# Moving the background modulation products out of two weight groups and into the first column blocks of the output projection

## The chip, the cores and the metric

The kernel runs on one core of one Trainium2 chip. The metric is the device time of one execution in microseconds (us); the core's TensorE (PE), VectorE (DVE), ScalarE (ACT), GpSimd (POOL) and the queue of SyncE (SP), which issues nearly all transfers, work side by side, each through its own instructions in a fixed order.

## What is computed

One layer of a streaming encoder on 512 tokens of width 2048, in float32. What matters here, cut from the reference:

```
cond = silu(c)
mod  = cond @ ada_w + ada_b                     # (2048,) @ (2048, 12288)
sh_m, sc_m, gt_m, sh_f, sc_f, gt_f = split(mod, 6)
h = rms_norm(x, mix_pre_g) * (1 + sc_m) + sh_m
(a_q ... d_v) = split(h @ w_in)                 # four mixers: delta rule, two attentions, spatial gate
y = concat(out_a, out_b, out_c, out_d) @ w_out  # output projection
x = x + gt_m * rms_norm(y, mix_post_g)
h = rms_norm(x, ffn_pre_g) * (1 + sc_f) + sh_f
x = x + gt_f * rms_norm(conv_glu_ffn(h), ffn_post_g)
```

## The kernel before, in words

Every large product is done in three matmuls of a split operand: a weight tile is loaded (`raw`, 512 KB to a unit), ACT rounds it to `hi`, DVE takes `lo = raw - hi`, and PE adds hi\*hi, lo\*hi and hi\*lo. Units come through `wunit` (line 351 is the load, 376 the `hi`, 377 the `lo`). Four `raw` tiles and five `hi`/`lo` pairs are in turn.

The kernel first makes `h` and the early groups of the input projection (keys, queries, values and gate of the delta rule). Then the delta rule itself runs (DeltaNet below: convolutions and norms at lines 787 to 856, a triangular solve by 31 steps of two DVE operations at lines 944 and 946, a recurrence over 8 chunks at 1006 to 1044), then come the late groups of the input projection in the order bv, bk, ck, dv, bq, cq, du (L380 to L382 and L573 to L575), the attentions of mixer B (L1107 to L1129) and mixer C (L1149 to L1187), and the output projection. That is the order of the program's text. A scheduler interleaves it: on each engine the text's order gives the priority, so the late groups' matmuls fill PE while the DeltaNet chain waits for DVE and ACT. What stands in which order on an engine is fixed when the kernel is built.

The modulation `mod` is worked in the background. Of its 24 column pieces the first 8 are needed at once; the other 16 (`bg_units(range(8, 24))`, the gates and the FFN's shift and scale) are cut into 9 steps each, 144 in all. Eight are units of 512 KB (`gemv_unit`: load at L415 into one of five tiles `ada`, which odd weight units of the late groups and the rows of x in the output projection share). Units 0, 2, 4, 6 make two products each on ACT (L430, L434), which POOL adds up (L435); units 1, 3, 5, 7 make two products each on DVE (L428, L432). The ninth step adds the two sums on DVE (L439) and stores them (L692).

Steps are called in two places. In the late groups `between()` does `pace[0]` steps per weight unit, set from the table `RATE`, one number for each of the seven groups; there are 8 units in bv, bk, dv, bq, cq and du, 4 in ck. In the output projection, four column blocks (`cb`) of 8 weight units each, `bg_step` is called once per unit. At the start of column block 0 and in unit 3 of blocks 0 to 2, `gate_row` loads a finished sum (L702) with a gain and a bias (L714, L715) and spreads it by two matmuls (L705, L706) into `gt`, by which the block's result is multiplied (`yg`, L1262) before it is stored (L1263).

Of the kernel before, what the change touches and what calls it, by code (L numbers as in the profile page):

```python
# [249 lines left out]
def trunk_kernel(ctx: ExitStack, tc: tile.TileContext, a: dict, out: bass.AP):  # L250
# [30 lines left out]
    def mt(s="m", shape=(P, 512), dt=F32):  # L281
        return cur[0].tile(list(shape), dt, tag="m", name=nm(s))
# [7 lines left out]
    def acc(s="acc"):  # L290
        return pp.tile([P, 512], F32, tag="acc", name=nm(s))
# [56 lines left out]
    def wunit(src, nk, w, own=True, shadow=False):  # L348

        raw = wraw() if own else araw()  # L350
        nc.sync.dma_start(out=raw[:, :nk * w], in_=src[:, :nk * w])
        step = max(1, 512 // w)
        out_ = []
        for j in range(0, nk, step):
            m = min(step, nk - j) * w
            hi = wp.tile([P, 512], F32R, tag="hi", name=nm("hi"))
            lo = wp.tile([P, 512], F32R, tag="lo", name=nm("lo"))
            split(raw[:, j * w:j * w + m], hi[:, :m], lo[:, :m], None, shadow)
            out_ += [(hi[:, i * w:(i + 1) * w], lo[:, i * w:(i + 1) * w]) for i in range(min(step, nk - j))]
        return out_  # L360
# [45 lines left out]
    def galloc(s, dt=F32):  # L406
        if mixing_open[0]:
            return gp.tile([P, 512], dt, tag="ga", name=nm(s), bufs=NGA)
        return mt(s, dt=dt)
# [299 lines left out]
    def gate_row(c, w, o):  # L709

        ps = bg_row(c)
        gt, pg = rtile("gt"), rtile("pg")
        sl = slice(o * 512, (o + 1) * 512)
        nc.sync.dma_start(out=gt, in_=a["gtb"][:, w * D + o * 512:w * D + (o + 1) * 512].partition_broadcast(P))  # L714
        nc.sync.dma_start(out=pg, in_=a["mpg" if w == 0 else "fpg"][0:1, sl].partition_broadcast(P))  # L715
        V.tensor_tensor(gt, gt, ps, ALU.add)
        V.tensor_tensor(gt, gt, pg, ALU.mult)
        return gt
# [21 lines left out]
    def bg_step(n=1):  # L740
        for _ in range(n):
            f = next(bg, None)
            if f is None:
                return
            bgn[0] += 1
            f()
# [20 lines left out]
    def late_groups(name, rate):  # L767
        pace[0] = rate
        for g in late:
            if (g[1][0][0] if g[0] == "FM" else g[1]) == name:  # L770
                if g[0] == "FM":
                    fm_group(g, ev_late_fm)
                else:
                    tm_group(g, ev_late_tm)

    def staged(name, j):
        t = mt("sd")
        nc.sync.dma_start(out=t, in_=std[STG[name] + j])
        return t
# [267 lines left out]

    late_groups("bv", RATE[0])
    late_groups("bk", RATE[1])
    late_groups("ck", RATE[2])  # L1050
    late_groups("dv", RATE[3])

# [41 lines left out]

    late_groups("bq", RATE[4])
    for tt in range(NTT):
# [36 lines left out]
    ckt = [staged("ck", j) for j in range(2)]  # L1133
    late_groups("cq", RATE[5])
    alit = [mt("ali") for _ in range(2)]
# [58 lines left out]
    def load_mix(uk):  # L1194
        raw = wraw()
        nc.sync.dma_start(out=raw.rearrange("p (k t) -> p k t", k=2), in_=mixd[uk[0]:uk[0] + 2].rearrange("k p t -> p k t"))
        for j, kt in enumerate(uk):
            mh[kt], ml[kt] = hslot(kt, "m")
            split(raw[:, j * 512:(j + 1) * 512], mh[kt], ml[kt])
# [5 lines left out]
    def turn(ygs, tag=None):  # L1205

        for j in range(4):
            ps = pp.tile([P, 512], F32, tag=tag or mtag(), name=nm("hT"), bufs=2)
            for tt in range(NTT):
                TE.transpose(ps[:, tt * P:(tt + 1) * P], ygs[tt][:, j * P:(j + 1) * P], ident)  # L1210
            t = mt("ygT")
            S.activation(t, ps, AF.Copy)
            ygT.append(t)

    def x_sums(cb):

        xs = []
        for tt in range(NTT):
            if tt % 2 == 0:
                xw = araw()  # L1220
            xr = xw[:, tt % 2 * 512:(tt % 2 + 1) * 512]
            nc.sync.dma_start(out=xr, in_=a["x"][tt * P:(tt + 1) * P, cb * 512:(cb + 1) * 512])
            jk = galloc("jx")
            S.activation(jk, xr, AF.Square, accum_out=sy[:, 3, tt * 4 + cb:tt * 4 + cb + 1])
            xs.append(xr)
        return xs
# [3 lines left out]
    for cb in range(4):  # L1230
        gt = gts.pop(0)
        ps = None
        us = gout[cb]
        ws = {}
        for n_, (ui, (uk, uc)) in enumerate(us):
            if cb == 0 and not 8 <= uk[0] < 12:
                load_mix(uk)
            for kt, w in zip(uk, wunit(a["w_out"][ui], len(uk), 512)):
                ws[kt] = w
            if ps is None:  # L1240
                ps = [acc("y") for _ in range(NTT)]
            if n_ == 3 and cb < 3:
                gts.append(gate_row(9 + cb, 0, cb + 1))
            if n_ == 1 and prev:
                turn(prev)
            if n_ == 1:
                xs = x_sums(cb)
            if not (cb == 3 and n_ > 3):
                bg_step(2 if cb < 2 else 3)
            if n_ == len(us) - 2 and cb == 3:  # L1250
                continue
            order = [(kt, tt) for kt in uk for tt in range(NTT)]
            if n_ == len(us) - 1 and cb == 3:
                order = [(kt, tt) for tt in range(NTT) for kt in us[n_ - 1][1][0] + uk]
            for kt, tt in order:
                sl = slice(tt * P, (tt + 1) * P)
                tm_mm(ps[tt], mh[kt][:, sl], ml[kt][:, sl], ws[kt][0], ws[kt][1], kt == korder[0], kt == korder[-1])
        prev = []
        for tt in range(NTT):
            i = tt * 4 + cb  # L1260
            yg = mt("yg")
            V.tensor_tensor(yg, ps[tt], gt, ALU.mult)  # L1262
            nc.sync.dma_start(out=ygd[tt, cb], in_=yg)  # L1263
            jk = galloc("jy")
            S.activation(jk, ps[tt], AF.Square, accum_out=sy[:, 0, i:i + 1])
            V.scalar_tensor_tensor(tt_("jz"), xs[tt], 1.0, yg, ALU.mult, ALU.mult, accum_out=sy[:, 2, i:i + 1])
            S.activation(jk, yg, AF.Square, accum_out=sy[:, 1, i:i + 1])
            prev.append(yg)
        if cb == 1:
            while bgn[0] < 12 * 9:  # L1270
                bg_step()
            S.activation(st(1), epst, AF.Sqrt)
        if cb == 2:
            for c in range(12, 20):
                ff_row(c)
            ff_cols()
# [335 lines left out]
    for ui, (uk, uc) in gdn[0]:  # L1612
        raw = wraw()
        nc.sync.dma_start(out=raw, in_=a["w_dn"][ui])
        for j in range(2):
            f, cb = (uk[j], uc[0] // 512) if len(uk) == 2 else (uk[0], uc[0] // 512 + j)
# [46 lines left out]
SHADOW = (0, 1, 2, 3)  # L1663
NHL2 = 3
NADA = 5
RATE = (1, 1, 2, 2, 3, 3, 3)
NGA = 3
NBR = 5
HV = (1, 4)
# [19 lines left out]
```

## Time and profile before

| what | value |
|---|---|
| time, median of 3 runs | 2326.64 us (2321.76 to 2336.99) |
| the profiled execution's own time | 2319.29 us |
| its span | 2316.8 us |
| PE busy | 2189.0 us, 94% of the span |
| DVE, ACT, POOL busy | 73%, 63%, 46% |
| DMA | 480.24 MB, mean 207 GB/s |

The span is from the first to the last instruction; 2.5 us of the execution's time lie outside it. Busy time is summed over the whole kernel; PE's matmuls overlap, so that a busy PE is an upper bound of its work. The background steps run between 176 us and 803 us of the span; behind that comes the FFN, which the change does not touch.

### The profile page before, as it was taken

How to read it: one execution, taken by the hardware profiler on the slowest of the kernel's cores; microseconds unless marked ns; L12 is line 12 of the kernel's file. 1: busy time of each engine (PE TensorE's matmuls, PEld its weight loads, DVE VectorE, ACT ScalarE, POOL GpSimd, SP SyncE). 2: the span in 40 equal slices, each digit the busy share in tenths (PEclk: the TensorE clock that was granted, in tenths of full speed). 3: DMA queues.
4: the chain of work that ended last, by engine and by line, in shares of the span. 5: the costliest groups of instructions: out<-in, count | busy, mean ns of one | idle time of the engine just before them, and what ended most of it. 6: DMA issues, size and time to landing. Idle time of an engine off the chain costs nothing. (4 is left out here: it accounts for less than half of the span.)

```text
span 2316.8 us, 31339 instructions
## 1 busy us (share of the span) xinstructions
PE 2189.0 (94%) x9852; PEld 1734.0 (75%) x9852; DVE 1680.9 (73%) x2665; ACT 1463.4 (63%) x2638; POOL 1077.0 (46%) x848
## 2 busy tenths in 40 slices
PE   5999999989999998989999999999999999999998
PEld 3878876767677786767788887777777777877776
DVE  5887678877878545956665568788788767777777
ACT  5767465355567544666777677776776677666663
POOL 4663032243323200256445465755765765564643
PEclk8999999999999999999999999999999999999999
DMA  8876555677888754678853547456545634435333
GB/s 299 285 259 236 170 183 180 198 240 254 295 306 284 248 171 146 231 257 291 282 206 137 182 167 273 160 198 213 190 176 204 216 141 173 155 106 194 119 132 137
DMA packets 206574, 480.24 MB, mean 207 GB/s; under 512 B 32692, under 2 KB 74180, under 8 KB 206408
## 3 DMA queue, kind: packets, MB, share of 16 engines
q1 hardware_dynamic: 199576, 477.19, 59.1%
q10 hardware_dynamic: 6832, 1.06, 0.2%
q8 instruction: 78, 1.28, 0.2%
q14 instruction: 88, 0.72, 0.1%
HBM read 399.50 MB, written 78.67 MB: 206 GB/s over the span
## 5 line engine op out<-in xcount | busy, mean ns | idle before, releaser
L1481 PE MATMUL X<-hi,ah 128*128 128x512 f32 x960 | 386.8, 403 | 19.3 <-DVE c L1493 6.1
L435 POOL TENSOR_TENSOR ga<-ga,ada 128x512 f32<-128x512 f32 (+1 forms) x167 | 226.5, 1356 | 369.5 <-ACT ada L434 348.9
L1482 PE MATMUL X<-lo,ah 128*128 128x512 f32 x960 | 383.7, 400 | 1.0 <-DVE lo L1447 1.0
L1483 PE MATMUL X<-hi,al 128*128 128x512 f32 x960 | 383.4, 399 | 0.0
L1447 DVE TENSOR_TENSOR lo<-raw,hi 128x512 fp32r<-128x512 f32 x360 | 264.2, 764 | 110.7 <-ACT hi L1446 110.2
L1468 POOL TENSOR_TENSOR raw<-raw 128x512 f32<-128x512 f32 x120 | 161.9, 1353 | 319.3 <-ACT hi L1443 232.1
L1481 PE MATMUL Z<-hi,ah 128*128 128x512 f32 x720 | 286.8, 398 | 6.4 <-ACT c L1491 2.9
L1444 DVE TENSOR_TENSOR lo<-raw,sh 128x512 fp32r<-128x512 f32 x360 | 240.1, 683 | 72.2 <-ACT sh L1442 35.6
L1442 ACT ACTIVATE sh<-raw 128x512 fp32r<-128x512 f32 x360 | 210.5, 588 | 124.1 <-DMA raw<-w_dn 63.3
L1483 PE MATMUL Z<-hi,al 128*128 128x512 f32 x720 | 285.7, 397 | 0.8 <-POOL al L1418 0.8
L1482 PE MATMUL Z<-lo,ah 128*128 128x512 f32 x720 | 285.4, 396 | 0.0
L1446 ACT ACTIVATE hi<-raw 128x512 fp32r<-128x512 f32 x360 | 214.4, 625 | 95.2 <-PE X L1483 36.4
L1443 ACT ACTIVATE hi<-raw 128x512 fp32r<-128x512 f32 x360 | 221.4, 622 | 35.7 <-PE Z L1483 24.9
L1481 PEld LDWEIGHTS X<-hi,ah 128*128 128x128 f32 x960 | 183.1, 191 | 66.5 <-DVE c L1493 7.4
L380 PE MATMUL acc<-hh,hi 128*128 128x512 f32 x544 | 221.3, 410 | 9.2 <-ACT lt L764 6.7
L382 PE MATMUL acc<-hh,lo 128*128 128x512 f32 x544 | 221.5, 410 | 4.2 <-DVE lo L374 4.1
L381 PE MATMUL acc<-hl,hi 128*128 128x512 f32 x544 | 222.4, 409 | 0.4 <-POOL hl L493 0.3
L1482 PEld LDWEIGHTS X<-lo,ah 128*128 128x128 f32 x960 | 183.0, 191 | 43.2 <-DVE lo L1447 1.3
L1483 PEld LDWEIGHTS X<-hi,al 128*128 128x128 f32 x960 | 183.0, 191 | 42.7
L1481 PEld LDWEIGHTS Z<-hi,ah 128*128 128x128 f32 x720 | 135.7, 189 | 41.2 <-ACT c L1491 4.3
L432 DVE SCALAR_TENSOR_TENSOR ga<-ada,cond,ga 128x512 f32<-128x512 f32 (+1 forms) x183 | 148.7, 813 | 22.2 <-DMA ada<-ada 20.3
L376 ACT ACTIVATE hi<-raw 128x512 fp32r<-128x512 f32 (+1 forms) x162 | 97.6, 609 | 100.3 <-PE y L575 51.7
(363 smaller groups left out, 4698.0 us busy)
## 6 DMA issues: line engine op xcount, KB each, us to landing
ada<-ada SPq DMA_DIRECT2D x184, 512.0 KB, 4.6
raw<-w_up SPq DMA_DIRECT2D x172, 512.0 KB, 5.9
raw<-w_dn SPq DMA_DIRECT2D x86, 512.0 KB, 5.4
raw<-w_in SPq DMA_DIRECT2D x56, 512.0 KB, 4.4
partd<-c SPq DMA_DIRECT2D x80, 256.0 KB, 4.2
c<-partd SPq DMA_DIRECT2D x80, 256.0 KB, 3.7
actd<-q SPq DMA_DIRECT2D x40, 512.0 KB, 3.3
ar<-actd SPq DMA_DIRECT2D x35, 512.0 KB, 3.5
```

What stands on the lines that cost most here:

```text
L380: TE.matmul(o, sh, mh, start=first, stop=False)
L381: TE.matmul(o, sh, ml, start=False, stop=False)
L382: TE.matmul(o, sl, mh, start=False, stop=last)
L435: G.tensor_tensor(accs[eng], accs[eng], src, ALU.add)
L1442: S.activation(sh, src, AF.Copy)
L1443: S.activation(h_, src, AF.Copy)
L1444: V.tensor_tensor(l_, src, sh, ALU.subtract)
L1446: S.activation(h_, src, AF.Copy)
L1447: eng.tensor_tensor(l_, src, h_, ALU.subtract)
L1481: TE.matmul(ps, ah[:, sl], wh, start=st_, stop=False, skip_group_check=True)
L1482: TE.matmul(ps, ah[:, sl], wl, start=False, stop=False, skip_group_check=True)
L1483: TE.matmul(ps, al[:, sl], wh, start=False, stop=sp_, skip_group_check=True)
```

## The change

Two numbers and one condition. In `RATE` the groups bv and bk go from 1 step per weight unit to 0, so 16 steps are no longer called there. In column blocks 0 and 1 of the output projection each unit calls 3 steps in place of 2, which is 16 more. Before, 112 steps were called in the late groups and 32 in the two column blocks; now it is 96 and 48. Either way the 144th is called in the last unit of column block 1, so the calls of blocks 2 and 3 find nothing left.

```
@@ -1246,7 +1246,7 @@
             if n_ == 1:
                 xs = x_sums(cb)
             if not (cb == 3 and n_ > 3):
-                bg_step(2 if cb < 2 else 3)
+                bg_step(3)
             if n_ == len(us) - 2 and cb == 3:
                 continue
@@ -1663,7 +1663,7 @@
-RATE = (1, 1, 2, 2, 3, 3, 3)
+RATE = (0, 0, 2, 2, 3, 3, 3)
 NGA = 3
```

Since all later calls go on from where the earlier ones stopped, the same call now does a step that is 16 earlier in the list, until the output projection catches up.

On DVE, in the norms of the DeltaNet keys (`cv` is the convolution of one head, `ga` the running sum of products, `lo` a weight split of a late group; what is before has -, what is now has +):

```order
 L856 TENSOR_TENSOR kq_2558<-cv_2587,nB_2605 128x2x128
 L787 TENSOR_SCALAR cv_2609<-pa_357,colp 128x512
-L377 TENSOR_TENSOR lo_3664<-ada_3657,hi_3663 128x512
 L790 SCALAR_TENSOR_TENSOR cv_2609<-pa_357,colp,cv_2609 128x511
+L377 TENSOR_TENSOR lo_3637<-ada_3630,hi_3636 128x512
 L790 SCALAR_TENSOR_TENSOR cv_2609<-pa_357,colp,cv_2609 128x510
-L377 TENSOR_TENSOR lo_3698<-raw_3695,hi_3697 128x512
 L790 SCALAR_TENSOR_TENSOR cv_2609<-pa_357,colp,cv_2609 128x509
-L432 SCALAR_TENSOR_TENSOR ga_3875<-ada_3958,cond,ga_3875 128x512 x2
+L377 TENSOR_TENSOR lo_3667<-raw_3664,hi_3666 128x512
 L792 SCALAR_TENSOR_TENSOR cv_2609<-pa_357,cv_2609 128x512
```

Two products are gone from between the four operations of one head's convolution, and the weight splits have moved a little.

On the SP queue, at the boundary of column blocks 0 and 1 (`ada<-ada` is a load of a background unit, `raw<-w_out` of a weight unit, `ygd<-yg` the store of a result of block 0), before:

```order
L351 DMA raw_7267<-w_out 128x1024
L351 DMA raw_7311<-w_out 128x1024
L351 DMA raw_7368<-w_out 128x1024
L351 DMA raw_7413<-w_out 128x1024
L714 DMA gt_6867<-gtb 128x512
L715 DMA pg_6868<-mpg 128x512
L415 DMA ada_7239<-ada 128x1024
L702 DMA ga_7321<-accd 128x512
L1263 DMA ygd<-yg_7101 128x512
```

and now:

```order
L351 DMA raw_7148<-w_out 128x1024
L1222 DMA ada_7186<-x 128x512 x2
L1222 DMA ada_7193<-x 128x512 x2
L415 DMA ada_7200<-ada 128x1024
L1263 DMA ygd<-yg_7064 128x512
L1263 DMA ygd<-yg_7072 128x512
L1263 DMA ygd<-yg_7080 128x512
L1263 DMA ygd<-yg_7088 128x512
L415 DMA ada_7206<-ada 128x1024
L351 DMA raw_7236<-w_out 128x1024
L415 DMA ada_7246<-ada 128x1024
L415 DMA ada_7252<-ada 128x1024
```

Before, the weights of block 1 were issued up to its sixth unit ahead of the first store; now its second unit is the last ahead of the stores, and its third comes behind the four of them.

## Rows read from the trace of the kernel before

**Rows 1.** The page: busy time of each engine.

```profile
PE 2189.0 (94%) x9852; PEld 1734.0 (75%) x9852; DVE 1680.9 (73%) x2665; ACT 1463.4 (63%) x2638; POOL 1077.0 (46%) x848
```

**Rows 2.** Busy time by stage: stretch, length, engines, granted PE clock, DMA share, GB/s.

```profile
176.00:264.00 88.00, 87.66 (x427) 72.91 (x426) 58.92 (x98) 50.14 (x86) 20.09 (x16) 1.00 0.59 203
264.00:423.00 159.00, 149.19 (x755) 113.19 (x754) 126.62 (x230) 85.61 (x132) 39.42 (x29) 0.98 0.54 176
423.00:488.00 65.00, 58.29 (x242) 46.52 (x241) 62.33 (x101) 25.78 (x42) 23.86 (x15) 0.95 0.69 236
...
583.00:692.00 109.00, 103.76 (x466) 77.87 (x465) 87.67 (x171) 63.68 (x134) 32.37 (x28) 1.00 0.86 307
692.00:764.00 72.00, 62.28 (x290) 48.20 (x289) 55.65 (x127) 49.11 (x111) 20.26 (x14) 0.95 0.76 266
764.00:813.00 49.00, 49.00 (x213) 39.18 (x212) 28.71 (x46) 26.77 (x56) 11.99 (x9) 0.97 0.82 267
813.00:912.00 99.00, 98.76 (x438) 78.84 (x437) 46.01 (x84) 45.18 (x105) 0.00 (x0) 1.00 0.51 160
```

**Rows 3.** What PE waited for from 264 to 488 us.

```profile
PE acc L380 <- ACT lt L764: 6.7, 1, 6.7
PE gF L922 <- DVE tg L920: 2.6, 2, 1.9
...
PE gB L889 <- DVE tl L887: 2.5, 1, 2.5
```

**Rows 4.** ACT in order of time, 452 to 484 us: start, length, instruction, idle before.

```profile
468.75 1.33 ACT L434 ACTIVATE ada<-ada,cond 128x512 f32<-128x512 f32 x2 [3.14 <-DMA ada<-ada]
...
471.92 1.58 ACT L764 ACTIVATE lt<-acc 128x512 f32<-128x512 f32 x3
```

**Rows 5.** Groups by line, 176 to 813 us: the background operations.

```profile
L432 DVE SCALAR_TENSOR_TENSOR ga<-ada,cond,ga 128x512 f32<-128x512 f32 x118 | 105.7, 896 | 17.2 <-DMA ada<-ada 16.2
...
L439 DVE TENSOR_TENSOR ga<-ga,ga 128x512 f32<-128x512 f32 x17 | 13.2, 775 | 3.5 <-POOL ga L435 3.0
...
L428 DVE TENSOR_SCALAR ga<-ada,cond 128x512 f32<-128x512 f32 x16 | 8.8, 547 | 2.8 <-DMA ada<-ada 2.7
...
L434 ACT ACTIVATE ada<-ada,cond 128x512 f32<-128x512 f32 x116 | 79.4, 715 | 43.2 <-DMA ada<-ada 31.0 <-DVE ga L432 7.0 <-DVE lo L377 3.1
...
L435 POOL TENSOR_TENSOR ga<-ga,ada 128x512 f32<-128x512 f32 x117 | 165.1, 1411 | 306.7 <-ACT ada L434 289.4 <-DVE ga L428 7.4 <-issue 3.1
```

**Rows 6.** Groups by line on DVE in the triangular solve, 423 to 488 us.

```profile
L432 DVE SCALAR_TENSOR_TENSOR ga<-ada,cond,ga 128x512 f32<-128x512 f32 x14 | 11.4, 818 | 0.0
...
L377 DVE TENSOR_TENSOR lo<-raw,hi 128x512 fp32r<-128x512 f32 x10 | 6.8, 684 | 0.1
```

**Rows 7.** What PE waited for from 692 to 813 us.

```profile
PE cT L1168 <- DVE cp L1063: 5.3, 7, 1.6
...
PE y L575 <- DVE ml L1187: 0.9, 1, 0.9
```

**Rows 8.** DVE in order of time at the end of column block 0.

```profile
760.97 0.69 DVE L716 TENSOR_TENSOR gt<-gt,gtps 128x512 f32<-128x512 f32 x1 [5.04 <-DMA gt<-gtb]
...
762.63 0.68 DVE L1187 TENSOR_TENSOR ml<-oc,mh 128x512 fp32r<-128x512 f32 x1
```

**Rows 9.** The SP queue in order of time there.

```profile
764.92 0.92 SPq L1263 DMA_DIRECT2D ygd<-yg  x2
...
767.34 0.92 SPq L1263 DMA_DIRECT2D ygd<-yg  x2
```

**Rows 10.** Transfers issued from 764 to 813 us: count, KB each, median us to landing.

```profile
ada<-ada SPq DMA_DIRECT2D x10, 512.0 KB, 3.6
raw<-w_out SPq DMA_DIRECT2D x8, 512.0 KB, 6.6
```

**Rows 11.** The fastest stretches for DMA in this part (columns as in rows 2).

```profile
660.00:690.00 30.00, 29.19 (x129) 21.79 (x128) 24.29 (x54) 19.48 (x43) 7.29 (x6) 1.00 0.91 323
...
680.00:692.00 12.00, 12.00 (x58) 9.41 (x57) 8.68 (x28) 7.46 (x21) 0.65 (x1) 1.00 1.01 364
```

More of the change, by code (lines that the diff above doesn't have):

```diff
@@ L1248, in trunk_kernel @@
             if not (cb == 3 and n_ > 3):
-                bg_step(2 if cb < 2 else 3)
+                bg_step(3)
             if n_ == len(us) - 2 and cb == 3:
@@ L1665 @@
 NADA = 5
-RATE = (1, 1, 2, 2, 3, 3, 3)
+RATE = (0, 0, 2, 2, 3, 3, 3)
 NGA = 3
```

## Prediction

> **What bounds the kernel now.** I read the page first: PE is busy for 94% of the span, far ahead of DVE and ACT [rows 1]. So the time is PE's work plus the places where PE waits, and a change that leaves PE's work alone, as this one does, can only move waits. The next view is the table by stage [rows 2]. Up to 264 us PE is busy for 87.66 of 88 us, and from 764 us for 49.00 of 49 and 98.76 of 99. Between them it is idle for 9.8 us in the preparation of DeltaNet (264 to 423), 6.7 us in the triangular solve (423 to 488), 5.2 us in mixer B and its neighbours (583 to 692) and 9.7 us in mixer C with column block 0 (692 to 764). DVE is the engine behind most of it: 62.33 of 65 us in the solve, 126.62 of 159 before it, 55.65 of 72 in block 0. Third, the table of who waited for whom: in the solve one wait of 6.7 us, for the eviction `lt` of group dv [rows 3]. In ACT's order of time that eviction stands behind two background products, for whose load ACT had been idle 3.14 us [rows 4]; so background work does hold up PE there, but these are steps of the groups ck and dv, whose rate is kept.
>
> The granted clock adds a little: 0.98, 0.95 and 0.95 in the three stages with the long waits, 1.00 where PE never stops [rows 2]. (1 - 0.95) of 65 us is 3.3 us of full-speed work lost around the 6.7 us wait, and 3.6 us are lost the same way in block 0. A wait taken away therefore gives back up to half as much again.
>
> **What is taken away.** Sixteen steps are one whole sum (eight units and its ninth step) and seven units of the next. On DVE that is 14 products, two of them first ones, and one addition: 12 x 0.896 + 2 x 0.547 + 0.775 = 12.6 us. On ACT 16 products x 0.715 = 11.4 us, on POOL 14 x 1.411 = 19.8 us [rows 5], and 15 loads of 0.524 MB, 7.9 MB. None of it is PE's. All later steps come 16 later, so in ck to du the number of steps per unit is the same as before and only the output projection makes up for it. The order shows this in DVE's queue, as products per section: up to the last DeltaNet norm 78 before and 62 now, from there to the solve 10 and 10, in the solve 16 and 18, from there to mixer B 30 and 30, in B 22 and 24, in C and the end of block 0 16 and 22, from block 0's results to block 1's 12 and 18. So what is taken away stood before the last norm (some 360 us).
>
> What is that worth? Up to 264 us nothing: PE does not wait. From 264 us on DVE had 32 us of idle time in 159 [rows 2], so a product less is a gain only where the chain of norms waits for it. The order tells how far: ahead of the last norm's matmul PE now has 1254 of the large matmuls, 1272 before, and 18 fewer at one per 0.23 us (49.0 us for 213 matmul rows in block 1 [rows 2]) are 4.1 us. DeltaNet comes to its solve 4.1 us earlier. In the solve DVE is full, and there it now has two products and one weight split more: 2 x 0.818 + 0.684 = 2.3 us [rows 6]. The solve's result is thus ready 4.1 - 2.3 = 1.8 us earlier, and ahead of its first matmul PE has the same 1739 large matmuls as before. **I take -2 us.** The ends: all 12.6 us come off PE's waits there (there are 9.8 + 6.7 = 16.5 us of them), or the freed time is lost in the solve, +2.3 us.
>
> **What is added in mixer C and block 0.** Six more products on DVE (5.4 us), but six weight splits (4.1 us) have moved ahead of mixer C, into B. DVE had 16 us idle in these 72 us, and PE's waits are for the softmax of mixer C, 5.3 us in seven pieces [rows 7], a chain that stands ahead of the background in priority. At the end of the block one thing changes for the better and one for the worse. Before, DVE sat idle 5.04 us for the bias row `gt` of the next block's gate, and `ml`, for which PE waited 0.9 us, stood behind it [rows 7, 8]; now that row is issued ahead of the last weights. But four products, of loads issued just before, now stand ahead of `ml`. **I take 0**, with -3 (that wait and its slow clock gone) and +4 (a product waits a whole landing, 3.6 us [rows 10], and `ml` behind it) as ends.
>
> **What is added in block 1.** This is the term that costs. Before, weights up to the sixth unit of block 1 were issued ahead of block 0's stores; now only two. The stores went out from 764.9 to 768.3 us [rows 9], and SP takes nothing else until they have their results. From there to the last unit's weights the queue now holds 15 background loads (7.9 MB), six weight units (3.1 MB), four stores (1.05 MB) and five rows of 0.262 MB (1.3 MB): 13.4 MB. The last unit's weights must be split some 6 us before 813 us (49 us for eight units is 6.1 us each), and landed a little before, say at 806. That is 13.4 MB in 37.7 us, 355 GB/s. The stage ran at 267 GB/s before; the best 30 us nearby ran at 323, the best 12 us at 364 [rows 2, 11]. At 364 it just fits; at 323 it takes 41.5 us and PE waits 3.8 us; at 267 it takes 50 us and PE waits 12.5 us. Demand is dense here, as it was in the stretch with 323, so **I take +4 us**, ends 0 and +12.5. DVE has room: 28.71 of 49 us were busy, and 6 x 0.9 us are added. Block 2 is nearly free of background loads (160 GB/s in 813 to 912 [rows 2]) and nothing of it is needed before mid block, so a late end of the list costs nothing behind block 1.
>
> The Trainium skill gives a ceiling for this (DMA: Bandwidth & Descriptors, Specifications): the HBM limit for one NeuronCore is about 358 GB/s. The trace's best 12 us, 364, agree with it to 2%, so nothing above that should be hoped for. If the queue ran at that ceiling all through block 1, 13.4 MB would take 37.4 us, the term would be 0 and the sum 4 us lower; no 30 us of this trace are that fast, so I keep the row's 323.
>
> **The sum.** 2319.3 (the profiled execution) - 2 + 0 + 4 = 2321.3. The median of the runs shown lies 7.3 us above the profiled one, so in runs as they are timed: **2328.6, say 2328 us**, no difference that can be measured (the runs of the kernel before are 0.65% apart, so a measurement tells about 1%, 23 us, from no change).
>
> **The rivals.** *DVE decides DeltaNet.* If the solve starts as much earlier as DVE has less ahead of it, 12.6 us, and the 6.7 us wait for `lt` goes, PE's waits from 264 to 488 shrink by 12.6 us and nothing is lost behind: 2326.6 - 12.6 = 2314. For it: DVE's 62.33 of 65 us. Against it: the products left at places where DVE was idle a fifth of the time, and the density in the solve goes up, not down. To be faster by over 1% the whole 16.5 us and the clock's 6.5 us of these two stages would have to go; chance 0.04.
>
> *The weights of block 1 come late.* SP serves its queue in order, and each weight unit now stands behind two or three background loads, each of which waits for one of five tiles to be freed. Below 355 GB/s PE waits; at the 267 GB/s of before for 12.5 us, and with the -2 of DeltaNet the time is 2326.6 + 10.5 = 2337. That is the slower side. For it: SP will have nothing to issue while it waits for block 0's results, and DVE and POOL must free the tiles. Against it: SP's queue moved 364 GB/s when asked to. Slower by over 1% needs some 215 GB/s there (13.4 MB in 62.7 us), under the rates shown for the stages from 423 to 813 us; chance 0.07.
>
> **How the numbers follow.** Forecast 0.62 (2320 to 2336, by its inner ends and the scatter of the runs), the DeltaNet rival 0.17, the late weights 0.21. The range takes in both rivals' times and a little of the scatter: 2312 to 2343. Faster by over 1% 0.04, slower by over 1% 0.07, between them 0.89.
>
> **What would show it.** In the profile after, PE idle from 264 to 488 us should be some 14.5 us (16.5 less 2), the last norm's matmuls 4 us earlier, and a wait for `lt` of the same order as before. In block 0 PE's waits for mixer C should stay near 5 us. In block 1, where there were none, PE should wait some 4 us for `lo` or `hi` of the last three or four units, with DMA above 300 GB/s. The forecast is wrong if block 1 has no wait at all (then the queue kept up), if PE's idle time in the solve changes by more than 5 us either way, or if waits turn up in mixer B, whose order has moved most (some 30 large matmuls more ahead of its last output) and for which I charge nothing.

## The result and the profile after

The changed kernel takes **2351.07 us** (median of 4 runs, 2345.39 to 2352.8) beside 2324.2 us for the kernel before in the same comparison: ratio **1.0106**, 95% interval 1.0082 to 1.013. It is 27 us slower; forecast were 2328 us and no change that can be measured. The profiled execution took 2350.59 us, its span is 2348.4 us. The page's row of busy times, which answers to [rows 1]:

```profile
PE 2197.9 (94%) x9852; PEld 1738.0 (74%) x9852; DVE 1700.3 (72%) x2665; ACT 1460.0 (62%) x2636; POOL 1082.3 (46%) x848
```

The instructions are as many as before, and DVE is busy 19 us longer with the same 2665 of them. That is the first sign of what happened: some of them take longer. The table by stage of the changed kernel, with the columns and stretches of [rows 2]:

```profile
264.00:423.00 159.00, 150.39 (x777) 115.68 (x777) 122.82 (x227) 82.13 (x128) 31.22 (x22) 1.00 0.46 151
423.00:488.00 65.00, 54.40 (x222) 43.32 (x222) 58.98 (x97) 24.78 (x41) 25.45 (x15) 0.89 0.70 229
...
583.00:692.00 109.00, 100.72 (x451) 75.21 (x451) 90.19 (x153) 60.54 (x122) 37.02 (x30) 1.00 0.77 285
692.00:764.00 72.00, 62.84 (x292) 48.76 (x291) 56.59 (x126) 44.24 (x105) 21.52 (x16) 0.98 0.76 270
764.00:813.00 49.00, 40.64 (x170) 30.60 (x168) 36.65 (x65) 30.74 (x72) 17.80 (x12) 0.90 0.78 267
813.00:912.00 99.00, 93.17 (x392) 72.83 (x393) 53.34 (x83) 47.06 (x102) 13.30 (x9) 0.98 0.70 240
```

Fixed stretches mix the stages once one kernel is late, so the next two tables cut each kernel at its own marks: the first matmul after the solve (L980), the last of the recurrence (L1044), the last of mixer B (L1126), the first results of column blocks 0 and 1 (the first and fifth L1262). Before:

```profile
500.00:581.30 81.30, 78.16 (x535) 61.69 (x536) 59.56 (x78) 46.22 (x82) 31.73 (x24) 1.00 0.71 249
581.30:675.40 94.10, 88.86 (x398) 66.12 (x397) 77.75 (x142) 53.91 (x110) 31.16 (x27) 1.00 0.84 300
675.40:764.20 88.80, 79.08 (x365) 61.51 (x364) 67.27 (x161) 59.33 (x135) 23.09 (x16) 0.96 0.79 277
764.20:812.90 48.70, 48.70 (x212) 38.89 (x212) 28.61 (x46) 26.57 (x56) 11.99 (x9) 0.97 0.82 267
```

And after:

```profile
499.70:590.50 90.80, 86.04 (x540) 67.85 (x541) 59.51 (x80) 46.18 (x82) 32.59 (x24) 0.92 0.66 228
590.50:692.50 102.00, 94.54 (x422) 70.53 (x421) 86.17 (x148) 57.04 (x115) 34.93 (x28) 1.00 0.79 292
692.50:784.00 91.50, 76.31 (x339) 58.17 (x338) 73.05 (x160) 57.24 (x134) 27.98 (x21) 0.93 0.76 266
784.00:841.60 57.60, 51.40 (x215) 39.65 (x214) 38.13 (x49) 29.11 (x60) 24.14 (x16) 0.96 0.81 284
```

The reader is to see three things. Up to 500 us nothing is lost (499.7 against 500.0). Then every stage is longer, by 9.5, 7.9, 2.7 and 8.9 us, 29 in all, to which column blocks 2 and 3 add 2.4. And the 29 us are mostly idle PE and low clock: PE is idle 1.6, 2.2, 5.5 and 6.2 us longer in the four stages, together 15.5; in the recurrence the clock is at the lower of its two levels, half of the other, for 10.2 us from 532.2 us on and 3.4 us from 576.5 on, which loses 6.8 us of full-speed work where none was lost, and mixer C and block 1 add some 3.4 us. PE's work is only moved: 24 matmul rows more lie in mixer B's stage (5.5 of its 7.9 us, at 0.23 each) and 26 fewer in mixer C's, which is therefore longer although it has less to do.

### The profile page after: what moved, and what is told of

The parts are those of the page before. It is cut to its first block, busy times and chain, and to the rows that moved or that the text cites. A ratio compares the mean times of both kernels' runs of the same rounds, so it can differ in the third digit from the quotient of the medians.

```text
span 2348.4 us, 31325 instructions
## 1 busy us (share of the span) xinstructions
PE 2197.9 (94%) x9852; PEld 1738.0 (74%) x9852; DVE 1700.3 (72%) x2665; ACT 1460.0 (62%) x2636; POOL 1082.3 (46%) x848
## 5 line engine op out<-in xcount | busy, mean ns | idle before, releaser
L435 POOL TENSOR_TENSOR ga<-ga,ada 128x512 f32<-128x512 f32 (+1 forms) x167 | 235.9, 1413 | 387.6 <-ACT ada L434 364.8
L1447 DVE TENSOR_TENSOR lo<-raw,hi 128x512 fp32r<-128x512 f32 x360 | 269.5, 779 | 107.9 <-ACT hi L1446 107.4
L380 PE MATMUL acc<-hh,hi 128*128 128x512 f32 x544 | 222.0, 411 | 13.0 <-ACT lt L764 10.6
L377 DVE TENSOR_TENSOR lo<-raw,hi 128x512 fp32r<-128x512 f32 (+1 forms) x162 | 123.1, 774 | 74.2 <-ACT hi L376 73.7
L432 DVE SCALAR_TENSOR_TENSOR ga<-ada,cond,ga 128x512 f32<-128x512 f32 (+1 forms) x183 | 155.3, 849 | 19.2 <-DMA ada<-ada 17.1
```

What stands on the lines that cost most here:

```text
L380: TE.matmul(o, sh, mh, start=first, stop=False)
L435: G.tensor_tensor(accs[eng], accs[eng], src, ALU.add)
L1447: eng.tensor_tensor(l_, src, h_, ALU.subtract)
```

## Why the early gain is gone at 500 us

The solve did start earlier, by 4.8 us (first L944 at 422.8 us before, 418.0 now). Then PE waited longer for the eviction `lt` of group dv than before [rows 3]:

```profile
PE acc L380 <- ACT lt L764: 10.6, 1, 10.6
```

ACT in order of time, with the idle time before each in brackets, tells why [rows 4]:

```profile
459.34 1.34 ACT L434 ACTIVATE ada<-ada,cond 128x512 f32<-128x512 f32 x2 [4.48 <-DMA ada<-ada]
...
467.80 1.33 ACT L434 ACTIVATE ada<-ada,cond 128x512 f32<-128x512 f32 x2 [6.08 <-DVE tmpi L944]
...
470.96 1.58 ACT L764 ACTIVATE lt<-acc 128x512 f32<-128x512 f32 x3
```

`lt` stands behind background products, and those behind loads and, by the second row, behind a step of the solve on DVE. It ran at 470.96 us, only 1 us earlier than before, although the solve had started 4.8 us earlier: PE spent most of what it had gained waiting for it, and the clock of this stage was 0.89.

## One wait in the recurrence, followed to its cause

Where does 0.92 in the recurrence come from? Three stretches of 10 us of the changed kernel, with the columns of the tables above:

```profile
520.00:530.00 10.00, 9.54 (x53) 7.37 (x51) 7.02 (x10) 5.89 (x9) 2.64 (x3) 1.00 0.85 292
530.00:540.00 10.00, 8.74 (x35) 6.84 (x36) 5.98 (x8) 2.97 (x5) 3.19 (x3) 0.61 0.53 189
540.00:550.00 10.00, 10.00 (x56) 8.17 (x56) 5.84 (x9) 4.33 (x8) 1.27 (x1) 0.88 0.61 195
```

The granted clock falls to the lower of its two levels (1.2 of 2.4 GHz) for most of the stretch from 530 to 540 us, and PE does 35 matmul rows there. Before, the same stretch has 66 of them at 1.00:

```profile
530.00:540.00 10.00, 10.00 (x66) 7.88 (x65) 7.71 (x10) 3.63 (x6) 5.01 (x4) 1.00 0.83 277
```

The clock falls at 532.2 us. Up to 531.26 us PE had stood idle for 1.72 us, for `o` of DVE:

```profile
531.26 0.66 PE L1044 MATMUL oT<-cst,o 128*128 128x128 f32 x4 [1.72 <-DVE o L1041]
```

DVE's operations on the way to that `o`, after (start, length):

```profile
527.07 0.69 DVE L1009 TENSOR_TENSOR u<-vt,pm 64x512 f32<-64x512 f32 x1
527.68 0.17 DVE L344 RECIPROCAL ro<-rod 128x4 f32<-128x4 f32 x1
527.77 1.76 DVE L1011 TENSOR_TENSOR sg<-S,egl 128x512 f32<-128x512 f32 x1
529.46 1.74 DVE L1041 TENSOR_TENSOR o<-o,ro 128x512 f32<-128x512 f32 x1
```

And before:

```profile
526.95 0.68 DVE L1011 TENSOR_TENSOR sg<-S,egl 128x512 f32<-128x512 f32 x1
...
528.41 0.69 DVE L1041 TENSOR_TENSOR o<-o,ro 128x512 f32<-128x512 f32 x1
```

The same two operations, 1.76 and 1.74 us long in place of 0.68 and 0.69. POOL in order of time says what differs. After:

```profile
527.41 3.24 POOL L435 TENSOR_TENSOR ga<-ga,ada 128x512 f32<-128x512 f32 x2 [7.26 <-ACT ada L434]
```

Before:

```profile
521.87 2.63 POOL L435 TENSOR_TENSOR ga<-ga,ada 128x512 f32<-128x512 f32 x2 [2.19 <-ACT ada L434]
529.46 3.07 POOL L435 TENSOR_TENSOR ga<-ga,ada 128x512 f32<-128x512 f32 x2 [4.96 <-ACT ada L434]
```

In the changed kernel two background additions of POOL lie beside both operations, 527.41 to 530.65 us; before, POOL was done at 524.50 us and began again when `o` was finished. Shifting the list of steps moved an addition by some microseconds, and it now lies on the chain. Nothing of it shows in an instruction count, and in DVE's queue only a product (L432), a weight split (L377) and a short reciprocal (L344) have changed places there.

The wait has its cause in these rows, but the clock has not. The kernel before has the same meeting of POOL with the same two operations later in its recurrence, with about the same wait behind it:

```profile
563.03 1.75 DVE L1041 TENSOR_TENSOR o<-o,ro 128x512 f32<-128x512 f32 x1
```

```profile
559.89 6.02 POOL L435 TENSOR_TENSOR ga<-ga,ada 128x512 f32<-128x512 f32 x4 [7.49 <-ACT ada L434]
```

```profile
564.83 0.66 PE L1044 MATMUL oT<-cst,o 128*128 128x128 f32 x4 [1.64 <-DVE o L1041]
```

There the clock stays at 1.00. Over the whole recurrence PE's waits for `o` are 3.1 us before and 3.3 after, and DVE is busy for 59.56 and 59.51 us. What the recurrence lost is thus above all the clock, and why it fell behind one of these waits and not behind the other no run shows.

The groups by line on DVE, 176 to 840 us, show the same over the whole stretch (`x` count | busy us, mean ns). Before (the row of L432 is in [rows 5]):

```profile
L377 DVE TENSOR_TENSOR lo<-raw,hi 128x512 fp32r<-128x512 f32 x97 | 68.9, 717 | 30.8 <-ACT hi L376 29.6 <-PE acc L382 0.8
...
L606 DVE TENSOR_TENSOR pa<-pa,acc 128x512 f32<-128x512 f32 x27 | 18.6, 687 | 20.9 <-PE acc L382 20.7
```

After:

```profile
L432 DVE SCALAR_TENSOR_TENSOR ga<-ada,cond,ga 128x512 f32<-128x512 f32 x117 | 111.6, 954 | 10.4 <-DMA ada<-ada 9.2
L377 DVE TENSOR_TENSOR lo<-raw,hi 128x512 fp32r<-128x512 f32 x84 | 67.7, 817 | 33.4 <-ACT hi L376 33.0
...
L606 DVE TENSOR_TENSOR pa<-pa,acc 128x512 f32<-128x512 f32 x28 | 19.2, 685 | 22.6 <-PE acc L382 22.6
```

A product takes 954 ns in the mean (896 before), a weight split 817 (717), and L606, which reads one operand from PSUM, 685 to 687 in both. Taken one by one in the kernel before, the 79 products that lie beside no work of POOL take 0.75 us, and the 38 that do lie beside some take 1.21 us in the mean and up to 1.87; of L606, 8 lie beside POOL and none of them takes over 0.69. The Trainium skill (SBUF — State Buffer, "SBUF: two separate sides") states that VectorE and GpSimd share one pair of ports to SBUF as an exclusive lock, which a VectorE operation with two SBUF inputs takes against a GpSimd operation that reads SBUF. The rows agree: with two SBUF inputs 0.69 us become up to 1.8, with one in PSUM nothing changes. The prediction took 0.896 as the price of a product and did not ask why it was not 0.75.

In block 1 the wait is the one that was forecast, late weights, and on SP's queue the longest waits are again for POOL, here for tiles that it still reads. PE's waits from 784 to 845 us, and those of the SP queue from 784 to 842 us (us in total, times, longest):

```profile
PE y L573 <- ACT hi L376: 4.5, 3, 2.2
```

```profile
SPq L415 <- POOL ga L435: 16.4, 7, 4.0
SPq L415 <- DVE ga L432: 5.6, 4, 2.0
```

The queue waited 22 us until POOL and DVE had freed a background tile, and moved 284 GB/s. Before, it waited 11.7 us for them in the 48.7 us of this stage, and moved 267.

## The experiments

All are edits of one of the two kernels; times are medians, ratios are to the kernel before, run beside them.

### Which part of the change costs, and whether the number of steps taken decides

```
e1_taken     RATE = (0, 0, 2, 2, 3, 3, 3), blocks 0 and 1: bg_step(2)
e2_added     RATE = (1, 1, 2, 2, 3, 3, 3), blocks 0 and 1: bg_step(3)
e3_bk_only   RATE = (0, 2, 2, 2, 3, 3, 3), blocks 0 and 1: bg_step(2)
e4_early     RATE = (2, 2, 2, 0, 3, 3, 3), blocks 0 and 1: bg_step(2)
```

> The rates of bv and bk are 0 as in the changed kernel, but column blocks 0 and 1 call 2 steps per unit as before; the last 16 steps then fall into block 2 (3 per unit). Up to column block 0 every engine's order is that of the changed kernel. Theory A (two separate losses: the steps taken out shift all later steps against the late groups, which costs from the recurrence to mixer C; three steps per unit cost in block 1): ratio to before 1.004 to 1.007, the stage from the solve's result to mixer C as long as in the changed kernel (some 10 us over before, a spell of slow PE clock in the recurrence included), block 1 back at 49 us. Theory B (the whole loss is in mixer C and the output projection; the slow clock in the recurrence was chance): ratio 0.998 to 1.002, no slow clock from 488 to 583 us.

> The rates of bv and bk are 1 as before, column blocks 0 and 1 call 3 steps per unit, so that the list ends after 11 units. Up to column block 0 every engine's order is that of the kernel before. Theory A: the stages up to mixer C as before, mixer C with block 0 some 5 us longer at most, block 1 between 47 and 51 us; ratio 1.000 to 1.003. Theory B: three steps per unit are the cause, so mixer C and block 0 lose the same 9 us as in the changed kernel; ratio 1.004 to 1.008.

> The 16 steps are all called in bk (rates 0 and 2), blocks 0 and 1 with 2 steps per unit; from ck on each call does the same step as before. Theory A: no shift against the late groups, so ratio 0.998 to 1.002. Theory C (any change of the list makes the scheduler place things anew, and what PE waits for from 488 to 764 us scatters by 10 us or more whatever the change means): the stages from 488 to 764 us differ by 5 us or more from before, either way.

> Rates 2, 2, 2, 0 for bv, bk, ck and dv: the same 112 steps in the late groups, but 16 more early, where DVE had a third of its time idle, and none in dv, whose eviction stood behind background products. Theory A: PE's wait for that eviction (6.7 us before) falls to under 2 us and its slow clock with it; ratio 0.994 to 0.998. Theory C: the gain there is lost or exceeded by scatter in the stages behind; ratio anywhere from 0.99 to 1.01.

Two more shift the list by other amounts:

```
e5_ahead2
-    late_groups("bv", RATE[0])
+    pace[1] = 2.0; late_groups("bv", RATE[0])
e6_behind18
-    late_groups("bv", RATE[0])
+    pace[1] = -2.0; late_groups("bv", RATE[0])
-RATE = (1, 1, 2, 2, 3, 3, 3)
+RATE = (0, 0, 2, 2, 3, 3, 3)
```

> Nothing is taken away: bv and bk keep their rate of 1, and the first weight unit of bv calls two steps more, so every later call does a step that is two further on in the list (instead of 16 further back). A sum has nine steps, so two ahead and sixteen behind put the same kind of step (even unit, odd unit, ninth step) at the same call. Theory PHASE (the loss of the change is a matter of which kind of step lies beside which operation of the recurrence, the mixers and block 0): it loses as the run with the steps only taken did, +12 to +22 us, 2338 to 2348, with a granted clock below 1.00 in the recurrence (500 to 590 us), which is 1.00 there before. Theory NUMBER (the loss comes of sixteen steps fewer ahead of the solve and sixteen left for later): two steps moved early cost nothing, 2326 within 6 us, clock 1.00 in the recurrence. Theory SCATTER (any change of the background makes a new order with a new loss): any time from 2326 to 2345, and no likeness to the changed kernel's shifts by stage.

> bv and bk call no step, as in the change, and the first unit of ck calls none in place of two; blocks 0 and 1 call two per unit as before and the last 18 steps are done in block 2. Every later call does a step that is 18 = two whole sums further back, so it is the same kind of step as before. Theory PHASE: as before or faster, 2315 to 2330, clock 1.00 in the recurrence, mixer C's end within 6 us of before. Theory NUMBER: at least as slow as with sixteen taken, +20 us or more, 2344 to 2352. Theory SCATTER: any time from 2326 to 2345.

Measured, with the lateness of the profiled execution against before at each mark (us). One execution of each kernel was profiled, up to 7.5 us off its median, so a few microseconds in one column mean little:

| kernel | median us | ratio, 95% interval | L980 | recurrence ends | mixer B ends | block 0 | block 1 | end |
|---|---|---|---|---|---|---|---|---|
| after | 2351.07 | 1.0106 (1.0082 to 1.013) | -0.3 | +9.2 | +17.2 | +19.8 | +28.8 | +31.5 |
| e1_taken | 2345.87 | 1.0093 (1.0065 to 1.0121) | +0.3 | +9.8 | +18.3 | +19.5 | +23.6 | +26.0 |
| e2_added | 2327.51 | 1.0002 (0.9985 to 1.0018) | -2.6 | -2.6 | -0.6 | -1.5 | -0.2 | +2.8 |
| e3_bk_only | 2325.7 | 0.9999 (0.9984 to 1.0013) | +3.6 | +1.9 | +11.3 | +2.2 | +2.8 | +10.6 |
| e4_early | 2344.4 | 1.0074 (1.0048 to 1.01) | -0.7 | +6.0 | +16.0 | +20.1 | +19.6 | +18.2 |
| e5_ahead2 | 2337.64 | 1.0058 (1.0041 to 1.0076) | +13.6 | +11.6 | +17.1 | +22.2 | +20.9 | +18.0 |
| e6_behind18 | 2347.02 | 1.0099 (1.0081 to 1.0116) | -0.9 | +7.8 | +16.1 | +17.2 | +17.7 | +26.2 |

The taken steps alone cost some 20 of the 27 us, with the same shifts up to block 0; e2, which only calls more steps per unit, costs nothing. For block 1 e2 says little: its list ends in the third unit there, after 8 steps, where the kernel before does 16 and the changed one 24. The third step there is what e1 lacks, and the changed kernel is 5.2 us slower than e1, with intervals that overlap. So my first theory, a fixed price for each part, is half right at best.

The number of steps taken does not decide: e4 and e5 do not take work away from before the mixers, they move it earlier, and lose 18 and 14 us, though e6 alone would fit that theory. Nor does the kind of step at each call: e6 has the kinds of before and loses as much as e1, and e5, with those of after, has a clock of 1.00 in the recurrence and loses in DeltaNet instead. Each order has a loss of its own, 0 to 27 us. The places are not all different, though: the changed kernel, e1, e4 and e6 lose 7 to 9.5 us in the recurrence and 8 to 10 in mixer B's stage, e5 loses ahead of L980 and in the mixers, and e3 gets back in mixer C what it loses in mixer B.

In e1 and e4, too, the first `o` of the recurrence takes 1.74 us beside POOL, PE waits 1.72 and 2.28 us for it, and the clock falls at 532.6 and 530.4 us; in e2, as in the kernel before, it is the third `o` that takes 1.75 us, PE waits 1.63 us, and the clock stays at 1.00. That is what a cause would do that depends on which two operations happen to coincide; these runs alone do not prove it.

### POOL's additions made short

```
-                G.tensor_tensor(accs[eng], accs[eng], src, ALU.add)
+                G.tensor_tensor(accs[eng][:, :64], accs[eng][:, :64], src[:, :64], ALU.add)
```

> The kernel before, with POOL adding only the first 64 of each 512 columns of the background products (the gates and the FFN's shift and scale are then sums of fewer units in the other columns). ACT's products, the loads, the waits between the engines and DVE's products stay. It is the measure for the next run. Theory POOL (POOL's additions make DVE's operations longer, 0.7 to 1.75 us, where they run at the same time, and this makes the waits): 5 to 15 us faster than before, since 12 such operations are in each of the stages with waits. Theory QUEUE (waits come of the order on DVE and ACT and of the loads, not of POOL): within 5 us of before.

> The changed kernel with POOL's additions cut to 64 of 512 columns in the same way; PE's order is the changed kernel's own, row for row. Theory POOL: most of the 25 us between the two kernels goes, the difference to the run before this one is under 8 us, the granted clock in the recurrence is 1.00 and the DVE operations of the recurrence take 0.7 us. Theory QUEUE: the difference stays at 18 us or more, with PE waiting at the same places.

| pair, after's edit less before's | before's | after's | difference | L980 | recurrence ends | mixer B ends | block 0 | block 1 | end |
|---|---|---|---|---|---|---|---|---|---|
| the kernels as they are | 2324.2 | 2351.07 | +26.9 | -0.3 | +9.2 | +17.2 | +19.8 | +28.8 | +31.5 |
| e7, e8: 64 columns | 2285.01 | 2289.39 | +4.4 | -1.4 | +0.2 | +7.0 | +5.0 | +7.2 | +6.0 |
| e9, e10: all on DVE | 2306.38 | 2323.45 | +17.1 | +5.3 | +4.9 | +9.2 | +12.9 | +11.9 | +12.0 |
| e11, e12: one in four on POOL | 2321.04 | 2330.21 | +9.2 | -0.2 | -6.1 | -11.4 | -6.1 | -3.4 | +1.0 |
| e13, e14: idle adds, early | 2368.44 | 2370.95 | +2.5 | -3.1 | -1.6 | -2.1 | -4.3 | -2.4 | +2.5 |
| e15, e16: idle adds, in place | 2325.64 | 2332.97 | +7.3 | +3.6 | +5.6 | +10.9 | +7.6 | +11.0 | +14.8 |

The two kernels leave out most of ACT's products from the sums. Both are far faster: 0.9837 (0.9817 to 0.9858) and 0.9838 (0.9818 to 0.9859) of before. The difference of their medians is 4.4 us and that of their means 0.3, neither clear of their scatter, though PE's order in e8 is the changed kernel's row for row. The cut gave 39 us to the one and 62 to the other. So the loss of this change, as it stands, needs POOL's long additions. The two operations of the recurrence in e8:

```profile
499.71 0.79 DVE L1011 TENSOR_TENSOR sg<-S,egl 128x512 f32<-128x512 f32 x1
500.43 0.68 DVE L1041 TENSOR_TENSOR o<-o,ro 128x512 f32<-128x512 f32 x1
```

DVE's groups by line in e8, beside those of after above:

```profile
L432 DVE SCALAR_TENSOR_TENSOR ga<-ada,cond,ga 128x512 f32<-128x512 f32 x114 | 86.2, 757 | 12.9 <-DMA ada<-ada 11.3
L377 DVE TENSOR_TENSOR lo<-raw,hi 128x512 fp32r<-128x512 f32 x107 | 73.2, 697 | 66.8 <-ACT hi L376 64.5 <-DMA ada<-ada 2.1
```

PE's wait for `lt` is 1.7 us here (10.6 in after), and the clock of the recurrence 1.00. From the first L980 to block 1's first result, in before, after, e7 and e8, one row from each kernel's table of stretches:

```profile
500.00:812.90 312.90, 294.80 (x1506) 228.21 (x1507) 233.19 (x423) 186.03 (x381) 97.97 (x75) 0.98 0.79 275
```

```profile
499.70:841.60 341.90, 308.29 (x1511) 236.20 (x1511) 256.86 (x435) 189.56 (x391) 119.64 (x88) 0.96 0.75 267
```

```profile
473.00:771.70 298.70, 291.95 (x1507) 228.88 (x1507) 201.47 (x423) 185.63 (x381) 30.71 (x75) 0.98 0.83 289
```

```profile
471.60:778.90 307.30, 295.61 (x1508) 231.81 (x1509) 210.89 (x434) 188.87 (x391) 40.34 (x87) 0.98 0.83 296
```

The third number in front of a bracket is DVE. After has 12 operations more than before there, 9 us at 0.75, and 23.7 us more busy time: the other 14.7 are lengthening. With POOL's additions short, 11 operations more are 9.4 us more, little over 11 at 0.75. And the same 423 operations of the kernel before take 31.7 us less. In the traces the cut gave 34 us to the kernel before, 27 of them ahead of 500 us (its first L980 comes at 473.0 us) and 14 between there and block 1's results, of which the stages behind gave 7 back.

### The same work without POOL, and with half of it

```
e9, e10
-                yield lambda c=c, i=i, accs=accs: gemv_unit(accs, (G, V)[i % 2], gada[c][i], i)
+                yield lambda c=c, i=i, accs=accs: gemv_unit(accs, V, gada[c][i], i)
e11, e12: (G, V, V, V)[i % 4] in that place; join() returns the one sum there is
```

> The kernel before with every background product of the late groups and the output projection on DVE (multiply and add in one operation of 0.75 us); ACT's products and POOL's additions of these units are gone, and nothing is left out of the sums. 64 units change sides, so DVE gets 128 operations of 0.75 us more, 96 us, and loses what POOL lengthened, some 51 us. Theory POOL: DVE has no lengthened operations left; the time is between 2300 and 2350, since 20 more products stand in the solve (15 us) where DVE is full. It is the measure for the next run. Theory QUEUE (the order on DVE and the loads decide): 2350 or more, as DVE has 45 us more to do.

> The changed kernel with every background product of these units on DVE. Theory POOL (the 25 us between the two kernels is POOL's additions beside DVE's operations): the difference to the run before this one is within 8 us either way. Theory QUEUE (products behind one another on DVE in the mixers and block 1): at least 18 us slower than the run before this one, since twelve more products now stand in mixer C and fourteen more in block 1. Theory SCATTER (each order has a loss of its own): any difference up to 20 us, of either sign.

> The kernel before with one unit in four (0 and 4 of a sum) on ACT and POOL and the other six on DVE: POOL's additions halve, and DVE gets 64 operations, 48 us, more. Theory POOL: half of the lengthening (25 us) goes, 2305 to 2335. Theory QUEUE: 2335 or more.

> The changed kernel with one unit in four on ACT and POOL. Theory POOL: the difference to the run before this one is about half of what it was, 8 to 15 us slower. Theory QUEUE: at least 18 us slower. Theory SCATTER: any difference up to 20 us, of either sign.

**e9 beats both kernels**: 2306.38 us, ratio 0.9925 (0.9898 to 0.9952), 20 us under before and 45 under after, with all of the computation in it. e10 is 0.9992 (0.9973 to 1.0012), e11 0.9978 (0.9959 to 0.9996), e12 1.0017 (0.9999 to 1.0035). The page's busy times of e9:

```profile
PE 2188.5 (95%) x9852; PEld 1735.5 (75%) x9852; DVE 1700.5 (74%) x2777; ACT 1378.9 (60%) x2508; POOL 916.1 (40%) x736
```

DVE got 128 products of 0.75 us and lost 16 additions of 0.775, 84 us on balance, and is busy only 20 us longer than before: 64 us of lengthening are gone. The half pair came out as the POOL theory said (9.2 us), though its two profiled executions are only 1.1 us apart, so that the table can't place the loss. The full pair did not: without one addition of POOL in the background, e10 is still 17 us slower than e9. There all 15 moved units are DVE's, 30 products in place of 14. The traces point to DVE's own work: it has 139 operations in the solve's stage (134 in e9) and 180 in mixer C's (168), where PE's wait for `cp` of DVE is 13.0 us in e10 and 9.0 in e9. No run parts this from the rest of the new order. So moved products can cost time without POOL, where a chain runs through DVE.

### Lengthening, or tiles held too long?

Short additions also free a background tile earlier. To part the two, POOL does scratch additions of 400 columns behind the short ones, on a tile that no other engine reads. The sums lack the same products as in e7 and e8.

```
e13, e14
+ G.tensor_tensor(dum, dum, dum, ALU.add)          # behind each 64-column addition
e15, e16
+ [G.tensor_tensor(dum, dum, accs[eng][:, :400], ALU.add) for _ in range(2) if j == 1 and w == 512]
```

> The kernel before with POOL's additions cut to 64 columns as in the run pool64_before, and behind each a second POOL addition of 400 columns on a scratch tile that no other engine reads or waits for. So POOL is busy at the same places about as long as before, but a background tile and the running sum are free as early as in pool64_before. Theory LENGTHENING (DVE's operations with both inputs in SBUF take longer while POOL works): most of the 39 us that the cut gave is lost again, 2310 to 2328. Theory HOLDING (what costs is that POOL holds the tiles, the running sum and with them SP's loads): it stays near pool64_before, 2285 to 2297.

> The changed kernel with the same two POOL additions. Theory LENGTHENING: 15 to 25 us slower than the run before this one, the granted clock in the recurrence falls again, L432 takes 0.9 us or more in the mean and a wait of PE for L1041 or S comes back. Theory HOLDING: within 8 us of the run before this one, both near 2290.

> In the two runs before, all scratch additions went to POOL's queue at the start, since nothing held them back, and cost 80 us there; from the first gate of DeltaNet on those kernels were as the cut ones. Here the two scratch additions of 400 columns read the running sum and stand behind the two 64-column additions of each unit, so POOL is busy where it is in the kernel before; a background tile is still free as soon as the 64 columns are added. Theory LENGTHENING: most of the 39 us that the cut gave is lost again, 2308 to 2330, and L432 takes over 0.85 us in the mean. Theory HOLDING: 2285 to 2300.

> The changed kernel with the same scratch additions in place. Theory LENGTHENING: 12 to 25 us slower than the run before this one, with the granted clock under 1.00 in the recurrence and in mixer C. Theory HOLDING: within 8 us of the run before this one.

The first pair missed its aim: the scratch additions depended on nothing, went to the front of POOL's queue, and cost 80 us before DeltaNet's first gate (354.8 us, 275.5 in the kernel before). From there on it repeats e7 and e8: ratios 1.0191 (1.0167 to 1.0215) and 1.0204 (1.0181 to 1.0227), 2.5 us apart, which is not clear of the scatter. The second pair has them in place. Two groups of e15, POOL's scratch additions and DVE's products:

```profile
L435 POOL TENSOR_TENSOR dum<-dum,ga 128x400 f32<-128x400 f32 x130 | 158.5, 1219 | 10.2
```

```profile
L432 DVE SCALAR_TENSOR_TENSOR ga<-ada,cond,ga 128x512 f32<-128x512 f32 x115 | 98.9, 860 | 12.0 <-DMA ada<-ada 11.2
```

e15 is as slow as the kernel before, 1.0 (0.9987 to 1.0013): all 40 us that the cut gave are lost again to additions that almost nobody waits for (DVE waits for them 3.1 us in all, at L439, where it waited 3.0 us for POOL before). Nor are the tiles held as before. SP's waits for POOL at the loads of background tiles, 264 to 842 us, in e7 and in e15:

```profile
SPq L415 <- POOL ga L435: 60.5, 29, 5.8
```

```profile
SPq L415 <- POOL ga L435: 58.6, 28, 6.1
```

In the kernel before they were 85.2 us. So POOL costs the kernel before its time by lengthening DVE's operations, not by holding tiles.

For the 27 us between the two kernels that is not shown. e16 is 1.0038 (1.0023 to 1.0052), 7.3 us over e15, which is less than the 12 to 25 us expected of lengthening and inside the 8 us expected of holding; nor is its clock below 1.00 in the recurrence. Its additions lie a microsecond or two beside those of the changed kernel, `o` (L1041) takes 0.841 us in the mean in place of 1.173, and the recurrence loses 2.0 us in place of 9.5. That fits a loss by coincidence, but a part by held tiles, above all in block 1, is not excluded.

## Why the prediction was wrong, point by point

- **DeltaNet, -2 us.** The solve started 4.8 us earlier (4.1 forecast), and its own length did not grow (64.3 us, 64.5 before; +2.3 forecast). By L980 0.3 us were left, since `lt` came only 1 us earlier. PE's idle time from 264 to 488 us was 19.2 us, where I had 14.5. I had read that `lt` waits behind background products [rows 4], and did not ask whether it would come earlier with the solve. An error of 1.7 us.
- **Mixer C and block 0, 0 us, ends -3 and +4.** +2.7 us, inside the ends, with 26 matmuls (6 us) fewer in the stage: PE's idle time (5.5) and the clock (2.6) cost 8 us more, PE's work 6 less.
- **Block 1, +4 us, ends 0 and +12.5.** +8.9 us, and the wait was the one named, `hi` of late weights. But the limit was not what the queue can move: the tiles were not free, and without POOL's long additions the stage loses 2.3 us (50.7 against 48.4). I had also read the queue's best too low. The 364 GB/s of [rows 11] is not the best 12 us of this trace, and the 358 that I took as a ceiling is none here: the measured rate decides, and the kernel before moved 407 GB/s in 12 us, and 376 in the 30 us from 5 to 35:

```profile
596.00:608.00 12.00, 10.66 (x61) 8.58 (x60) 11.30 (x27) 4.56 (x8) 2.70 (x3) 1.00 1.04 407
```

At 407 the 13.4 MB would have fitted with 5 us to spare; the term came out larger because of the tiles.
- **The failed step is what I left out: "waits turn up in mixer B, whose order has moved most ... and for which I charge nothing".** The recurrence (charged nothing, not even named) cost 9.5 us, 6.8 of it low clock, and mixer B 7.9, 5.5 of it matmuls moved there, which mixer C then lacked as cover. These 17 us and block 1 are the miss. I counted the products by engine and section, and took the stages with nearly equal counts (30 and 30, 22 and 24) as unchanged. The order behind the counts had changed, and with it which of POOL's additions lie beside which of DVE's operations on the chain: with the additions short the loss is not clear of the scatter (e7, e8). How much of the 17 us came this way stays open.
- **The rivals.** DVE did not give DeltaNet 12.6 us. The late weights (2337) were right in the place and too low in the time, as they were only a third of the loss.
- **The chances.** Slower by over 1% had 0.07. The orders shifted ahead of the mixers (the changed kernel, e1, e3 to e6) came out 0 to 27 us slower; a change that moves all later steps deserved a range that wide.

What stays open: how the 27 us divide between chance coincidences, of which the wait at 530 us is shown, tiles held longer, and DVE's own added products, whose cost is not clear of the scatter in e8 (0.3 to 4.4 us) and 17 us in e10, with twice as many of them. Nor does a run show that the 1.72 us wait brings the clock down: it, four small matmuls (L1044) and the start of eight more (L1016) are what PE did just before, but the recurrence before has a wait of 1.64 us for the same line later on, at a clock of 1.00.

## What to carry to other kernels

Work on one engine can lengthen the operations of another, so a mean duration over a group (0.896 us) can be a mixture of two prices (0.75 alone, up to 1.87 beside POOL); look for both before pricing a move, and see which of them stands on the chain that PE waits for. A list of filler steps that is shifted can change every later coincidence: here moving work out of a stage with slack gained nothing, and cost time in those that followed. And an offload to a slower engine should be tried both ways: here 0.75 us on DVE was cheaper than 0.715 us on ACT and 1.41 us on POOL, which lengthened DVE's other operations (e9).

## What the runs showed of the hardware

Beside a POOL addition of 128x512 from SBUF, DVE's operations of that size with two SBUF inputs took up to 1.8 us in place of 0.69 (products up to 1.87 in place of 0.75), and those with a PSUM operand stayed at 0.687. Over the stages from 500 to 813 us of the kernel before, making POOL's additions short took 31.7 us off DVE's 233, and it gave 39 us of the whole kernel's time, though POOL is hardly named in PE's waits. Additions put back where hardly anything waits for them (e15) cost all of it again. And 1.72 us of idle PE in the recurrence stood just ahead of 10 us with a granted clock of 0.61, in which PE got through 35 matmul rows in place of 66, while 1.64 us of idle PE in the recurrence of the kernel before were followed by a clock of 1.00; the clock took more from that stage (6.8 us) than the added idle time did (1.6).
